# Cumulative gate sums as TensorE products, and the scan's inverse blocks turned on VectorE and placed by Pool

## The chip, the core and the metric

The kernel runs on one core of one Trainium2 chip, in one launch. The metric is the device time of that core in microseconds: the median of repeated executions, 3512.65 us over three runs (3505.86 to 3517.88). One more execution was profiled; it took 3506.29 us. Engines are named as the profile names them: PE is TensorE's matmul row and PEld its weight loads, DVE is VectorE, ACT is ScalarE, POOL is GpSimd, SP is the queue that issues most DMAs.

## What is computed

Two layers of a diffusion trunk over 1024 latent tokens and 256 context tokens of width 1024, all in float32. Layer 0 mixes with pooling and neighbourhood attention, layer 1 with a bidirectional RWKV-7 recurrence; each is followed by a squared-ReLU MLP. The change lies in layer 1. For each direction and each of 16 heads of width 64 the reference does:

```
decay = exp(-exp(-softplus(-w_raw) - 0.5));  a = sigmoid(...);  k_d = k * (1 + (a - 1) * k_a)
S = S * w_t - (S kk_t) (kk_t * a_t) + v_t k_t        # one token after the other, context first
y_t = S r_t
...
bonus = sum(r * (k_d[0] + k_d[1]) * r_k, per head) * v
```

The recurrence is evaluated in chunks of 64 tokens. Within a chunk the decays enter through cumulative sums of their logarithms, and the coupling of a chunk's tokens through the inverse of a unit triangular 64x64 matrix, one for each chunk, direction and head.

## The kernel before

Layer 1's recurrence has two stages that the change touches.

**Features (`l1_scan_features`).** The work goes over 40 units `u`: five spans of 256 tokens (the context first, then four latent spans), each with eight groups of 128 channels (`hp`, two heads). The order is written out by hand, one iteration per unit, in which the steps of several units are interleaved: `decays(u+2)` puts the low-rank gate products on PE, `gates(u+2)` takes two tanh per direction on ACT (decay gate `sg`, key gate `th`; the reverse direction is written back to front) and adds 1 to `sg`, `norms(u+2)` spreads the key norms on PE, `sums(u+2)` forms the cumulative sum of `sg` over each chunk with a VectorE scan along 512 columns (line 1327; `smask` holds a 0 at each chunk's start) and scales the keys, `exps(u+1)` takes both exponentials on ACT, `keys(u+1)` scales the key gate on ACT, `scaled(u)` multiplies everything into the tile F on VectorE (lines 1357 to 1389) and stores it, `scores(u-1)` puts chunk products on PE and stores them to `ls`, and `bonuses(u-1)` adds the bonus sums (line 1413, two products of 2 columns a unit). Between them `value_mm`, `value_in` and `value_out` compute the value projection, 24 matmuls a unit. From the ninth unit on, 2.2 slots of the first inversions are taken from a generator in each iteration.

**The inversions (`scan_blocks`, `scan_invert`).** The diagonal 32x32 blocks of 2 chunks x 2 directions x 8 head pairs x 2 heads x 2 blocks are inverted together, 128 of them, one to a partition: tile M holds the blocks, X starts as identities, and 31 rounds of a product and a subtraction on VectorE (lines 1511 and 1515) leave the inverse. There are ten such blocks `b`; the first two are done during the features, the other eight in the background of the scan. Finished, X and a transposed copy of it (line 1518) are stored to the scratch tensors `lt` and `ltt`.

**Scan (`l1_scan`).** Twenty steps `s`, in each of which both directions `d` advance by one chunk. A step's PE work is a chain: `chain_x`, `chain_u`, `chain_s`, with the readouts and with the scores of the next step `n = s + 1` in four groups between them. A score group (line 1626) goes to one of three PSUM buffers of the pool `scps`, is copied in part by ACT (line 1632) and masked into ZQ by DVE (line 1634). The state SS is updated on DVE (lines 1734, 1738) and carried by ACT (line 1748). `load_blocks` and `load_inverses` fetch the inverses from the scratch: two loads a step for ZT (line 1595) and four for TT (line 1603), where 32 partitions hold a block's rows, so that each packet has 128 bytes. `compose1` and `compose2` (lines 1653, 1667) build the off-diagonal 32x32 part in PSUM of the pool `chps`, which has two buffers and also serves the chain.

What is not a step's own work comes from a generator `background()`: the inversions, then the loads and splits of the output weights and the first rows of the readout. `fill()` is called 16 times a step and draws `pace/2` slots: 2.1/2 until step 2, then 2.45/2, and 1/2 once the inversions are done. The loads of the next inversion (8 DMAs, line 1497) are issued at the 17th of a block's 31 rounds. Pools `M` and `X` have two buffers each; after the inversions their space takes output weights (`readout_weight`). All DMAs named here go through SP, in program order.

Of the kernel before, what the change touches and what calls it, by code (L numbers as in the profile page):

```python
# [58 lines left out]
class Trunk:  # L59
# [983 lines left out]
    def l1_features(self):  # L1043
# [14 lines left out]
        smask = cp.tile([128, 512], BF16, name="smask")  # L1058
        hb = cp.tile([128, 32], F32, name="hb")
        kac = cp.tile([128, 8], F32, name="kac")  # L1060
        rkbd = cp.tile([128, 8, 2], F32, name="rkbd")
# [3 lines left out]
        def scan_constants():  # L1065
            nc.vector.memset(smask, 1.0)
            nc.vector.memset(smask.rearrange("p (c t) -> p c t", t=CH)[:, :, 0:1], 0.0)
# [6 lines left out]
            for e in range(2):  # L1074
                s = slice(e * 64, e * 64 + 64)
                nc.vector.tensor_scalar(out=rkbd[s, :, e], in0=rk[s], scalar1=0.5, scalar2=None, op0=ALU.mult)
# [9 lines left out]
            self.sfc = smask, hb, kac, rkbd, sel, nln2  # L1086
# [108 lines left out]
    def l1_scan_features(self, es, xv, wv0):  # L1195
# [8 lines left out]
        knp = self.pool(es, "sfk", 1, PSUM)  # L1204
        bps = self.pool(es, "sfb", 1, PSUM)
        smask, hb, kac, rkbd, sel, nln2 = self.sfc
# [42 lines left out]
        def value_in(u):  # L1249
            vt = vp.tile([128, 256], F32, tag="vt", name="vt", bufs=1)  # L1250
            nc.scalar.copy(out=vt, in_=vps[u])
            vps[u] = vt

        def value_out(u):
# [5 lines left out]
            v = vp.tile([128, 2, 128], F32, tag="v", name="v", bufs=1)  # L1260
# [42 lines left out]
        def gates(u):  # L1303
# [4 lines left out]
            for d, ps in enumerate(w.pop("pw")):  # L1308
                for i, dst in ((0, sg), (1, th)):
                    c = 16 * i + d * 8 + hp  # L1310
                    nc.scalar.activation(
                        out=dst[:, d, ::-1] if d else dst[:, d], in_=ps[:, i], func=AF.Tanh, scale=0.5, bias=hb[:, c:c + 1]
                    )
            nc.scalar.activation(out=sg, in_=sg, func=AF.Copy, bias=1.0)
            w["sg"], w["th"] = sg, th

        def norms(u):
            t0 = units[u][0]
            ps = U[u]["kn"] = knp.tile([128, n], F32, tag="kn", name="kn")
            nc.tensor.matmul(out=ps, lhsT=sel[:, units[u][1]], rhs=self.rn[:, t0:t0 + n], start=True, stop=True)  # L1320

        def sums(u):
            w = U[u]
            hp = units[u][1]
            sg = w.pop("sg")
            w["cum"] = tp.tile([128, 2, n], F32, tag="cum", name="cum", bufs=2)
            nc.vector.tensor_tensor_scan(  # L1327
                out=fl(w["cum"]), data0=smask, data1=fl(sg), initial=0.0, op0=ALU.mult, op1=ALU.add
            )
# [4 lines left out]
        def exps(u):  # L1334
# [4 lines left out]
            nc.scalar.activation(out=pe[:, :, 1:], in_=cu(w["cum"]), func=AF.Exp, scale=-0.5 * DECAY)  # L1339
            nc.scalar.activation(out=w["cum"], in_=w["cum"], func=AF.Exp, scale=0.5 * DECAY, bias=nln2)  # L1340
# [8 lines left out]
        def scaled(u):  # L1349
# [6 lines left out]
            for d in range(2):  # L1356
                nc.vector.scalar_tensor_tensor(  # L1357
                    out=th[:, d], in0=th[:, d], scalar=1.0, in1=rv(kkt, d), op0=ALU.add, op1=ALU.mult
                )
            nc.vector.tensor_tensor(out=F[:, :, 2], in0=cu(th), in1=cu(iv), op=ALU.mult)  # L1360
            for d in range(2):
                cs = slice(d * nch, d * nch + nch)
                rk3 = (lambda x: c3(x)[:, ::-1, ::-1]) if d else c3
                nc.vector.tensor_tensor(out=F[:, cs, 1], in0=rk3(kkt), in1=pe[:, cs, 0:CH], op=ALU.mult)  # L1364
            for d in range(2):
                nc.vector.tensor_tensor(out=kd[:, d], in0=kd[:, d], in1=rv(w["x"][:, 0], d), op=ALU.mult)
            for d in range(2):
                cs = slice(d * nch, d * nch + nch)
                kap = F[:, cs, 3, ::-1] if d else F[:, cs, 3]
                nc.vector.tensor_tensor(out=kap, in0=c3(kd[:, d]), in1=c3(iv[:, d]), op=ALU.mult)  # L1370
# [15 lines left out]
            if lat:  # L1386
                ks = w["ks"] = tp.tile([128, n], F32, tag="ks", name="ks", bufs=1)
                nc.vector.tensor_tensor(out=ks, in0=kd[:, 0], in1=rv(kd[:, 1], 1), op=ALU.add)
# [17 lines left out]
        def bonuses(u):  # L1406
            w = U.pop(u)
            t0, hp = units[u]
            if w["lat"]:
                if hp == 0:  # L1410
                    self.bp = lps.tile([128, 2, 16], F32, tag="bp", name="bp")
                for j in range(2):
                    nc.tensor.matmul(
# [836 lines left out]
```

## Time and profile before

| | us |
|---|---|
| median of three runs | 3512.65 |
| profiled execution | 3506.29 |
| its span, first to last instruction | 3504.5 |
| PE busy | 3280.3 (94%) |
| PEld busy | 2737.5 (78%) |
| DVE busy | 2043.3 (58%) |
| ACT busy | 1439.4 (41%) |
| POOL busy | 307.6 (9%) |

The page gives shares over the whole span; the two stages of the change are 1859 to 2174 us and about 2184 to 2637 us of it, and there VectorE is far fuller than 58%. A row of instructions reads: line, engine, operation, tile written and tiles read, shape, count, then busy time and mean duration, then the idle time of the engine ahead of them and who ended it. A row of stretches gives for each engine the busy time and the number of instructions, then the clock that TensorE was granted, the busy share of the 16 DMA engines and what they moved.

### The profile page before, as it was taken

How to read it: one execution, taken by the hardware profiler on the slowest of the kernel's cores; microseconds unless marked ns; L12 is line 12 of the kernel's file. 1: busy time of each engine (PE TensorE's matmuls, PEld its weight loads, DVE VectorE, ACT ScalarE, POOL GpSimd, SP SyncE). 2: the span in 40 equal slices, each digit the busy share in tenths (PEclk: the TensorE clock that was granted, in tenths of full speed). 3: DMA queues.
4: the chain of work that ended last, by engine and by line, in shares of the span. 5: the costliest groups of instructions: out<-in, count | busy, mean ns of one | idle time of the engine just before them, and what ended most of it. 6: DMA issues, size and time to landing. Idle time of an engine off the chain costs nothing. (4 is left out here: it accounts for less than half of the span.)

```text
span 3504.5 us, 62351 instructions
## 1 busy us (share of the span) xinstructions
PE 3280.3 (94%) x25466; PEld 2737.5 (78%) x25466; DVE 2043.3 (58%) x3903; ACT 1439.4 (41%) x2743; POOL 307.6 (9%) x396
## 2 busy tenths in 40 slices
PE   8999989999999999989997877899998899999998
PEld 4787767888888889867887776788887788888887
DVE  4255555343444444486757989799766734444446
ACT  4244456312121212166767665566664531221212
POOL 0010110000001000013530000000021100000000
PEclk9999999999999999999999888899999999999999
DMA  8432243322222211143226777898883411111112
GB/s 280 150 94 88 90 137 124 104 76 87 79 79 91 79 43 43 43 141 95 79 70 177 232 229 230 182 209 205 227 219 120 157 48 49 46 46 47 49 49 78
DMA packets 462189, 409.10 MB, mean 117 GB/s; under 512 B 151584, under 2 KB 401312, under 8 KB 461904
## 3 DMA queue, kind: packets, MB, share of 16 engines
q1 hardware_dynamic: 449024, 368.22, 36.0%
q0 software_dynamic: 10560, 35.14, 2.9%
q8 instruction: 200, 3.28, 0.4%
q10 hardware_dynamic: 2320, 1.77, 0.2%
q14 instruction: 85, 0.70, 0.1%
HBM read 292.54 MB, written 112.49 MB: 116 GB/s over the span
## 5 line engine op out<-in xcount | busy, mean ns | idle before, releaser
L916 DVE TENSOR_TENSOR yacc<-yps,yacc 128x512 f32<-128x512 f32 x540 | 369.7, 690 | 304.1 <-PE yps L93 303.7
L74 ACT CAST wh<-st 128x1024 fp32r<-128x1024 f32 x160 | 165.1, 1049 | 761.3 <-PE yps L93 557.8
L93 PE MATMUL yps<-wh,xh 128*128 128x512 f32 x1152 | 453.2, 393 | 3.2 <-DVE yacc L916 1.5
L93 PE MATMUL yps<-wh,xl 128*128 128x512 f32 x1152 | 448.6, 390 | 0.7 <-DVE xl L75 0.7
L93 PE MATMUL yps<-wl,xh 128*128 128x512 f32 x1152 | 449.0, 390 | 0.0
L75 DVE TENSOR_TENSOR wl<-st,wh 128x1024 fp32r<-128x1024 f32 x160 | 194.3, 1229 | 278.2 <-ACT wh L74 278.1
L93 PE MATMUL acc<-h2h,wh 128*128 128x426 f32 (+3 forms) x768 | 274.4, 357 | 3.0 <-ACT y L671 3.0
L93 PE MATMUL acc<-h2h,wl 128*128 128x426 f32 (+3 forms) x768 | 273.3, 356 | 0.0
L93 PE MATMUL acc<-h2l,wh 128*128 128x426 f32 (+3 forms) x768 | 273.0, 355 | 0.0
L93 PEld LDWEIGHTS yps<-wh,xh 128*128 128x128 f32 x1152 | 216.2, 188 | 71.2 <-DVE yacc L916 12.1
L93 PEld LDWEIGHTS yps<-wh,xl 128*128 128x128 f32 x1152 | 216.2, 188 | 47.8 <-DVE xl L75 2.3
L93 PEld LDWEIGHTS yps<-wl,xh 128*128 128x128 f32 x1152 | 216.4, 188 | 44.7 <-issue 1.7
L898 DVE TENSOR_TENSOR r<-r 128x428 f32<-128x428 f32 (+4 forms) x164 | 102.4, 624 | 240.2 <-ACT r L897 240.2
L93 PE MATMUL acc<-mh,wh 128*128 128x256 f32 (+1 forms) x640 | 215.6, 338 | 4.3 <-ACT mh L74 4.2
L93 PE MATMUL acc<-ml,wh 128*128 128x256 f32 (+1 forms) x640 | 214.8, 336 | 0.0
L93 PE MATMUL acc<-mh,wl 128*128 128x256 f32 (+1 forms) x640 | 214.1, 335 | 0.0
L93 PE MATMUL acc<-h2bh,wh 128*128 128x512 f32 (+3 forms) x544 | 211.3, 388 | 1.4 <-ACT wh L74 0.7
L93 PE MATMUL acc<-h2bl,wh 128*128 128x512 f32 (+3 forms) x544 | 211.1, 388 | 1.3 <-DVE h2bl L288 1.3
L93 PE MATMUL acc<-h2bh,wl 128*128 128x512 f32 (+3 forms) x544 | 210.8, 388 | 0.3 <-DVE wl L75 0.3
L897 ACT ACTIVATE r<-acc 128x428 f32<-128x428 f32 (+4 forms) x164 | 89.1, 543 | 291.0 <-PE acc L93 272.0
L93 PEld LDWEIGHTS acc<-h2h,wh 128*128 128x128 f32 x768 | 144.2, 188 | 15.9 <-issue 5.1
L1626 PE MATMUL sc<-FT 64*128 64x192 f32 (+1 forms) x1280 | 144.6, 360 | 11.3 <-DVE ZQ L1641 4.9
(319 smaller groups left out, 6849.5 us busy)
## 6 DMA issues: line engine op xcount, KB each, us to landing
st<-in_mlp_w SPq DMA_DIRECT2D x128, 512.0 KB
ft<-F SPq DMA_DIRECT2D x64, 512.0 KB
FT<-ft SPq DMA_DIRECT2D x128, 256.0 KB
adas<-in_ada_w POOLq DMA_DIRECT2D x112, 256.0 KB, 3.9
adas<-in_ada_w SPq DMA_DIRECT2D x80, 256.0 KB
x<-x SPq DMA_DIRECT2D x28, 512.0 KB
bias<-in_bias SPq DMA_DIRECT2D x64, 192.0 KB
ls<-ls SPq DMA_DIRECT2D x80, 128.0 KB
```

Of the source, the lines that this page charges most:

```text
L74: self.nc.scalar.copy(out=hi, in_=src)
L75: self.nc.vector.tensor_tensor(out=lo, in0=src, in1=hi.bitcast(F32), op=ALU.subtract)
L93: self.nc.tensor.matmul(out=ps, lhsT=lhs[x], rhs=rhs[y], start=first and i == 0, stop=last and i == 2)
L897: nc.scalar.activation(out=r, in_=ps, func=AF.Relu)
L898: nc.vector.tensor_tensor(out=r, in0=r, in1=r, op=ALU.mult)
L916: nc.vector.tensor_tensor(out=yacc[t][:, n], in0=ps, in1=yacc[t][:, n], op=ALU.add)
L1626: nc.tensor.matmul(out=p4[:, j, e, f], lhsT=F[st[e], 2 * g + j, 3:5].rearrange("p a t -> p (a t)"), rhs=F[st[e], 2 * g + j, f], start=True ...
```

## The change

Features: the decay gate is turned on PE in four 128x128 transposes, the +1 is added by ACT on the way back from PSUM, and four float32 products with a triangle of ones (two 64x64 triangles on the diagonal of `tri`) give the sums, straight in the channels' layout. The exponentials read them from PSUM. The bonus is accumulated over the eight channel groups in one PSUM tile of 16 rows, and turned at the end. The key gate `th` is no longer written back to front; instead the products of `scaled` read it reversed, and those of both directions are merged where they can be. `keys(u+1)` moves behind `scores`, `bonuses`, `turned` and `norms`.

```diff
+        def turned(u):
+            sg = fl(U[u]["sg"]).rearrange("p (b t) -> p b t", t=128)
+            ps = bps.tile([128, 4, 128], F32, tag="tr", name="sgt")
+            for b in range(4):
+                nc.tensor.transpose(out=ps[:, b], in_=sg[:, b], identity=self.ident)
+            nc.scalar.activation(out=sg, in_=ps, func=AF.Copy, bias=1.0)
         def sums(u):
-            nc.vector.tensor_tensor_scan(
-                out=fl(w["cum"]), data0=smask, data1=fl(sg), initial=0.0, op0=ALU.mult, op1=ALU.add
-            )
+            ps = w["sum"] = cmp.tile([128, 2, n], F32, tag="cum", name="cum")
+            for b in range(4):
+                nc.tensor.matmul(out=fl(ps)[:, b * 128:(b + 1) * 128], lhsT=sg[:, b], rhs=tri, start=True, stop=True)
...
-            for d in range(2):
-                nc.vector.scalar_tensor_tensor(
-                    out=th[:, d], in0=th[:, d], scalar=1.0, in1=rv(kkt, d), op0=ALU.add, op1=ALU.mult
-                )
-            nc.vector.tensor_tensor(out=F[:, :, 2], in0=cu(th), in1=cu(iv), op=ALU.mult)
+            nc.vector.scalar_tensor_tensor(out=th, in0=th, scalar=1.0, in1=both(kkt), op0=ALU.add, op1=ALU.mult)
...
+                nc.vector.tensor_tensor(out=F[:, cs, 2], in0=rk3(th[:, d]), in1=c3(iv[:, d]), op=ALU.mult)
...
-                for j in range(2):
-                    nc.tensor.matmul(
-                        out=self.bp[:, j, 2 * hp:2 * hp + 2], lhsT=w["ks"][:, j * 128:(j + 1) * 128], rhs=rkbd[:, hp], start=True, stop=True
-                    )
+                nc.tensor.matmul(out=fl(self.bp)[0:16], lhsT=rkbd[:, hp], rhs=w["ks"], start=hp == 0, stop=hp == 7)
```

Scan: only the first two blocks still go through the scratch, read in eight loads each. From the third on, X itself is kept in `ready` and turned by two VectorE block transposes at the start of step `2b - 1`, the step before the block is first used (`n = 2b`). Pool copies the turned rows into TT at the start of each step; ZT is a view. A block's partitions are ordered anew, so that its loads are 16 of 8 partitions. `compose2` takes its PSUM from `scps`.

```diff
-                for d in range(2):
-                    p0 = t * 64 + bl * 32 + d * 16
-                    dma(out=M[p0:p0 + 16], in_=self.ls[b // 2, d, :, :, blk, (2 * b + t) % 4, blk].rearrange("h e s t -> (h e) s t"))
+                for e in range(2):
+                    for d in range(2):
+                        p0 = e * 64 + bl * 32 + t * 16 + d * 8
+                        dma(out=M[p0:p0 + 8], in_=self.ls[b // 2, d, :, e, blk, (2 * b + t) % 4, blk])
...
+            def turn_inverses(b):
+                X = ready.pop(b)[1]
+                rows = ip.tile([128, 32, 32], F32, tag="BK", name="YR")
+                columns = zs.tile([128, 32, 32], F32, tag="YC", name="YC", bufs=1)
+                nc.vector.transpose(out=columns.rearrange("p m r -> p r m"), in_=X)
+                nc.vector.transpose(out=rows.rearrange("p m t -> p t m"), in_=X.rearrange("p r t -> p t r"))
+            def place_inverses(s):
+                for q in range(4):
+                    bl = q % 2
+                    nc.gpsimd.tensor_copy(out=dh(TT[quads[q], :, :, bl * 32:bl * 32 + 32]), in_=rows[quads[q]])
...
-                p2 = chps.tile([128, 2, 8, 32], F32, tag="ch", name="p2")
+                p2 = scps.tile([128, 2, 512], F32, tag="sc", name="p2")[:, 0].rearrange("p (d h t) -> p d h t", d=2, h=8)
...
                     for i, _ in enumerate(self.scan_invert(ip, b, *blocks)):
-                        if i == 16 and b + 1 < NSTEP // 2:
-                            blocks = self.scan_blocks(ip, b + 1, nc.sync.dma_start)
+                        if i >= 16 and nxt is None and b + 1 < NSTEP // 2 and b - 1 not in ready:
+                            nxt = self.scan_blocks(ip, b + 1, nc.sync.dma_start)
                         yield
+                    ready[b] = blocks
+                    while nxt is None and b + 1 < NSTEP // 2:
+                        if b - 1 not in ready:
+                            nxt = self.scan_blocks(ip, b + 1, nc.sync.dma_start)
+                        yield
...
-                self.readout_weight_load(0)
...
-                for k in (1, 2, 3):
+                for k in (0, 1, 2):
                     self.readout_weight_load(k)
...
-                self.readout_weight(1)
+                while ready:
+                    yield
+                for k in range(2):
+                    self.readout_weight(k)
+                    yield
...
                     load_values(n, d)
+                    if not d and n % 2 == 0:
+                        while n >= 4 and n // 2 not in ready:
+                            next(bg)
+                        first_inverses(n // 2) if n < 4 else turn_inverses(n // 2)
+                    if not d and s:
+                        place_inverses(n)
                     chain_x(s, d)
```

More of the change, by code (lines that the diff above doesn't have):

```diff
@@ L1085, in scan_constants @@
             nc.vector.memset(nln2, -LN2)
-            self.sfc = smask, hb, kac, rkbd, sel, nln2
+            self.sfc = tri, hb, kac, rkbd, sel, nln2
         self.open_wpool(es, 1, 2)
@@ L1203, in l1_scan_features @@
         lps = self.pool(es, "sfl", 1, PSUM)
-        knp = self.pool(es, "sfk", 1, PSUM)
+        cmp = self.pool(es, "sfc", 1, PSUM)
         bps = self.pool(es, "sfb", 1, PSUM)
-        smask, hb, kac, rkbd, sel, nln2 = self.sfc
+        tri, hb, kac, rkbd, sel, nln2 = self.sfc
         half = (slice(0, 64), slice(64, 128))
@@ L1311, in gates @@
                     nc.scalar.activation(
-                        out=dst[:, d, ::-1] if d else dst[:, d], in_=ps[:, i], func=AF.Tanh, scale=0.5, bias=hb[:, c:c + 1]
+                        out=rv(dst[:, d], d and i == 0), in_=ps[:, i], func=AF.Tanh, scale=0.5, bias=hb[:, c:c + 1]
                     )
-            nc.scalar.activation(out=sg, in_=sg, func=AF.Copy, bias=1.0)
             w["sg"], w["th"] = sg, th
@@ L1434, in l1_scan_features @@
                 gates(u)
+                turned(u)
+                sums(u)
                 norms(u)
-                sums(u)
-            exps(0)
+                scaled_keys(u)
+                if u == 0:
+                    exps(u)
             keys(0)
@@ L1464, in l1_scan_features @@
                 if u + 2 < nu:
+                    turned(u + 2)
                     norms(u + 2)
+                if u + 1 < nu:
+                    keys(u + 1)
                 if v < nu:
@@ L1581, in load_values @@
                 W[s]["D"][d] = D_
-            quarter = lambda x, s, bl, e: x.rearrange("(s b c e) i t -> i s b e c t", s=2, b=2, e=2)[:, s % 2, bl, e]
+            quads = [slice(q * 32, q * 32 + 32) for q in range(4)]
+            turned, ready = {}, {}
             def load_blocks(s, e):
@@ new lines, in first_inverses @@
+            def first_inverses(b):
+                rows, columns = ip.tile([128, 32, 32], F32, tag="BK", name="YR"), zs.tile([128, 32, 32], F32, tag="YC", name="YC", bufs=1)
+                for t, src in ((rows, lt_[b]), (columns, ltt_[b])):
+                    for q in quads:
+                        nc.sync.dma_start(out=t[q], in_=src[q].rearrange("m i t -> i m t"))
+                turned[b] = rows, columns
+            def turn_inverses(b):
[4 more added lines that the diff above has]
+                nc.vector.transpose(out=rows.rearrange("p m t -> p t m"), in_=X.rearrange("p r t -> p t r"))
+                turned[b] = rows, columns
@@ L1793, in l1_scan @@
                 nc.gpsimd.memset(W[0]["D"][d][0:64], 0.0)
+            first_inverses(0)
             for e in range(2):
                 load_blocks(0, e)
-                load_inverses(0, e)
+            nc.gpsimd.memset(TTs[1], 0.0)
+            for s in range(2):
+                place_inverses(s)
             for d in range(2):
```

98 lines of the change are left out of this document (50 added, 48 removed).

## The prediction, made before the changed kernel was run

> **What bounds the kernel now.** I read the page first, then the trace by stage. The change touches two stages: the RWKV features (about 1859 to 2174 us, 40 units of 256 tokens by 128 channels) and the scan (about 2184 to 2637 us, 20 steps). The busy times by stretch are context units, latent units, scan steps with the inversion behind them, and scan steps after it:
>
> ```profile
> core 0: us, PE busy (x) PEld busy (x) DVE busy (x) ACT busy (x) POOL busy (x), PEclk, DMA share, GB/s
> 1859.00:1907.00 48.00, 43.32 (x500) 40.08 (x499) 42.75 (x92) 43.65 (x98) 1.93 (x10) 1.00 0.69 209
> 1907.00:2174.00 267.00, 210.06 (x2157) 191.44 (x2155) 248.27 (x607) 169.87 (x379) 6.45 (x34) 0.90 0.76 225
> 2284.00:2500.00 216.00, 197.37 (x4915) 175.58 (x4916) 197.09 (x491) 140.18 (x270) 4.43 (x8) 0.95 0.87 204
> 2500.00:2616.00 116.00, 107.53 (x2749) 95.71 (x2744) 77.53 (x101) 82.96 (x154) 28.08 (x12) 0.96 0.89 241
> ```
>
> Units are counted by the one key activation that each has, in the same two feature stretches:
>
> ```profile
> L1347 ACT ACTIVATE kd<-th,kac,cols 128x512 f32<-128x512 f32 x9 | 7.3, 816 | 0.8 <-DVE F L1370 0.8
> L1347 ACT ACTIVATE kd<-th,kac,cols 128x512 f32<-128x512 f32 x32 | 26.1, 814 | 44.6 <-DVE ks L1388 35.7 <-DMA FT<-ft 6.3 <-DVE ks L1389 2.2
> ```
>
> A latent unit thus takes 267/32 = 8.35 us, in which VectorE (DVE) works 248.3/32 = 7.76 us (93%) and TensorE (PE) 6.56 (79%): VectorE bounds it. A context unit takes 48/9 = 5.33, and there TensorE is the fullest together with ScalarE (43.3 and 43.7 of 48). In the scan TensorE and VectorE are both at 91% while the inversion runs. After it VectorE falls to 67%, yet TensorE stays at 93%, so TensorE is the scan's floor. A step's length does not fall when VectorE empties: nine state updates, two to a step, lie between 2405.0 and 2495.1, which is 90.1/4 = 22.5 us a step.
>
> ```profile
> L1738 DVE TENSOR_TENSOR SS<-SS,pcs x9: 691/692/693, 2405.0 to 2495.1; 128x512 f32<-128x512 f32 x9
> L1515 DVE TENSOR_TENSOR X<-X,tmp 128x112 f32<-128x112 f32 (+15 forms) x183 | 63.1, 345 | 6.3
> L1511 DVE TENSOR_TENSOR tmp<-X,M 128x112 f32<-128x112 f32 (+15 forms) x183 | 62.2, 340 | 2.9
> L1634 DVE TENSOR_TENSOR ZQ<-sc,masks 128x512 f32<-128x512 f32 x79 | 54.0, 685 | 8.7 <-ACT TM L1632 8.6
> L1518 DVE COPY M<-X 128x1024 f32<-128x1024 f32 x6 | 6.4, 1062 | 0.1
> ```
>
> **Features: the sums move to TensorE.** The scan leaves VectorE. Of a unit on TensorE these rows show the small work, in order of time, ahead of the value projection:
>
> ```profile
> L1327 DVE TENSOR_TENSOR_SCAN cum<-smask,sg 128x512 f32<-128x512 bf16 x40 | 48.8, 1220 | 6.1 <-ACT sg L1314 5.4
> ...
> 1994.05 0.44 PE L1259 MATMUL vtr<-ident,vt 128*128 128x128 f32 x2 [1.46 <-ACT vt L1251]
> 1994.42 1.15 PE L1398 MATMUL lp<-F 64*64 64x64 f32 x32
> 1995.50 0.61 PE L1413 MATMUL bp<-rkbd,ks 128*128 128x2 f32 x4
> 1995.96 0.36 PE L1320 MATMUL kn<-rn,sel 128*128 128x256 f32 x1
> 1996.16 0.28 PE L93 MATMUL acc<-mh,wh 128*128 128x256 f32 x1
> ```
>
> Removed: 1.22 us of VectorE a unit. The merged products over both directions save about 0.15 more (estimate: two pairs of 256 columns become single ones of 512, while one of 512 is split). VectorE would need 7.76 - 1.37 = 6.4 us in a latent unit. Added on TensorE: four transposes and four f32 products against the triangle, 128 columns each. Two transposes hold the queue 0.37 us up to the next group, so four about 0.6. The bonus product shows what an f32 product with full 128x128 weights costs: four instructions in 0.46 us, 0.115 each, two instructions a product. The triangle's products have 128 moving columns instead of 2; 0.115 is the lower bound and 0.185 the upper (a transpose of 128 columns, 0.37/2, the change to the next group counted in). I take 0.115, since eight products in a row change group only once: 8 x 0.115 = 0.9, and 1.5 at the upper bound. The new bonus product (two passes of 256 columns, 16 weight columns) costs about what the old four instructions did. Sum: 0.6 + 0.9 = 1.5 us a unit. Everything else in this stage goes together at nothing: the +1 on ScalarE has the same size from PSUM, the norm product only changes its pool, the value copies share a ring, and the mask's fills give way to two small DMAs.
>
> So what is late next is TensorE. Latent units: busy 6.56 + 1.5 = 8.06, from which the pipelined tails go (the rows above start 0.1 to 0.2 before the one ahead ends, in five groups, so up to 0.8): 7.3 to 8.06; I take 7.75 and gain 0.6 x 32 = 19 us. Context units: 43.3/9 = 4.8 busy of 5.33, 0.5 is free, so 1.5 - 0.5 = +1.0 each, 9 units: +9 us. The bounds are +4 and +13.
>
> **The block loads double.** A 64x64 inverse block is now read by 16 DMAs of half the size where 8 were, on the same SP queue. Two of the stalls that such loads cause today, once in the features and once in the scan:
>
> ```profile
> 2056.18 4.45 SPq L1497 DMA_DIRECT2D M<-ls  x8
> 2064.76 0.19 DVE L1511 TENSOR_TENSOR tmp<-X,M 128x31 f32<-128x31 f32 x1 [5.35 <-DMA xt<-ascr]
> 2201.23 5.27 SPq L1497 DMA_DIRECT2D M<-ls  x8
> 2209.69 0.19 DVE L1511 TENSOR_TENSOR tmp<-X,M 128x31 f32<-128x31 f32 x1 [6.84 <-DMA M<-ls]
> ```
>
> Eight issues take 4.45 us, 0.55 each, and VectorE goes on 3.2 to 4.1 us after the last. Sixteen take 8.9, so data are there 12 to 13 us after the first issue instead of 8.5. In the features this lengthens two stalls of VectorE by 4.4 each: +9 us at most, if nothing absorbs it. Features in all: -19 + 9 + 9 = -1 us.
>
> **Scan: the inverses no longer go through the scratch.** Removed from SP: six loads a step (TT and ZT) and two stores a block; from the DMA engines, the smallest packets:
>
> ```profile
> DMA packets 172289, 94.94 MB, mean 210 GB/s; under 512 B 120481, under 2 KB 160373, under 8 KB 172193
> ...
> TT<-lt SPq DMA_DIRECT2D x78, 64.0 KB
> ...
> M<-ls SPq DMA_DIRECT2D x64, 64.0 KB
> ...
> ZT<-ltt SPq DMA_DIRECT2D x39, 64.0 KB
> ```
>
> TT and ZT are 117 x 512 = 59,904 packets of 128 bytes, half of the small ones. Added on VectorE: two block transposes of 128x1024 a block for one transposing copy of 1.06 us (the L1518 row). I price each like that copy, net +1.06 x 8 blocks = 8.5 us, between 0 and twice that; it sits at the start of a step, ahead of the masks, and VectorE has 22.5 - 20 = 2.5 us free in such a step (below), so 0 to 4 us end up on the path; I take 1. The Trainium skill, "VectorE: DVE Perf Modes", section "The three transpose paths", gives 311 ns for 128x128 in bf16 on VectorE; eight of them would be an estimated 2.5 us a transpose, and by that the net would be 3.9 us a block. No run here shows it.
>
> What can be gained is bounded by TensorE's idle time from 2284 to 2616: 18.6 + 8.5 = 27 us. The rows that the change removes from it:
>
> ```profile
> PE p L1667 <- DVE SS L1734: 9.6, 6, 2.4
> ...
> 2303.53 5.93 DMA FT<-ft
> 2309.47 5.08 DMA TT<-lt
> ...
> 2502.39 7.73 DMA FT<-ft
> ```
>
> The second composition moves to the score pool, so it no longer waits for a state update queued behind the inversion: up to 9.6. The DMA pieces in the chain are 18.7 us, mostly beside busy engines; I take a third. Together -16.
>
> **The new wait.** X is now kept until its block is turned, X has two buffers, and so the loads of block b+1 wait for the turn of block b-1, which happens at the start of step 2b-3. The schedule is static: 16 fills a step at 1.225 background slots, 19.6 a step, 32 slots a block. Counting slots through the loop: today the loads are issued 16 slots before the inversion that needs them, and the last block ends in step 13. With the change blocks 6 to 9 start two slots after their loads (steps 7, 9, 11, 13) and block 5 four slots after (step 5); the last ends in step 14. Two slots are under 2.5 us, the loads need 12. I place the first issue 2.5 us into the step (behind the outputs, values and keys that SP sends there), so data are there at 14.4. VectorE arrives after the turn (2 x 1.06) and two masks (2 x 0.685), at about 5.5: it stands still for 9 us. Queued behind on VectorE: the masks of the third and fourth score group, the state updates, all later inversion. Waiting for those: the score buffers (three), ScalarE's carry of the state and with it all its copies. TensorE has work until it needs the third group's buffer again. These are the ends of one half step of the chain, which has the first composition inside that the half with the wait does not have:
>
> ```profile
> 2383.73 1.08 PE xp L1678 x32
> 2384.81 1.50 PE sc L1626 x16
> ...
> 2387.39 1.13 PE p L1653 x64
> ...
> 2392.46 0.85 PE sc L1626 x8
> ```
>
> Such a half lasts 9.58 - 1.13 = 8.45 us; with the next xp (1.08) and one score group (0.75) TensorE needs the buffer at 10.3. It gets it at 14.4 + two short inversion pairs (0.19 a product, 0.8) + 0.69 = 15.9. That is 5 us for each of four blocks, and 3 for block 5, whose start leaves two slots more: +23, and no fewer than 0. In return the inversion is spread over two steps a block instead of 1.6: VectorE's load falls from 22 to 8 x 0.685 + 4 x 0.69 + (31 x 0.685 + 2.1)/2 = 20 us a step, which is why the lag does not pile up.
>
> **POOL's copies.** Four copies of 32x512 a step go to Pool, which has nothing to do there. Their length is between the memset rate and that of its two-input rows, 0.5 to 1.2 us each: half of its 1.05 us for a 128x1024 memset, and half of 2.36 (row below); half a step covers them. Three rows speak of a cost elsewhere: the same 128x128 subtraction on VectorE, once beside a Pool operation and once alone.
>
> ```profile
> L1501 POOL MEMSET X<- 128x1024 f32 x7 | 7.3, 1047 | 239.2 <-DMA lt<-X 104.4 <-DVE ZQ L1641 63.8 <-DVE X L1515 35.5
> ...
> 2607.35 2.36 POOL L1990 TENSOR_TENSOR y<-y,ld 128x1024 f32<-128x1024 f32 x1 [6.34 <-DVE gst L1933]
> 2607.71 2.15 DVE L75 TENSOR_TENSOR gs<-gst,gs 128x128 fp32r<-128x128 f32 x1 [0.36 <-ACT gs L74]
> 2630.43 0.29 DVE L75 TENSOR_TENSOR gs<-gst,gs 128x128 fp32r<-128x128 f32 x1 [3.26 <-ACT gs L74]
> ```
>
> The first ended with Pool's operation, 1.9 us late. The inversion's operations are of that kind (two inputs from SBUF), so four copies could hold VectorE 2 to 4.8 us a step. In the five steps with the new wait that is hidden; in ten others VectorE's 2.5 us free cover most: +3. The Trainium skill, "SBUF — State Buffer", section "SBUF: two separate sides", says that a Pool operation and a VectorE one with two SBUF inputs lock each other out for the whole instruction; the rows agree.
>
> **Ends.** At the start SP has 38 issues ahead of the first step's values instead of 34 (8 first loads and 8 more block loads, 12 fewer TT/ZT): 4 x 0.55, +2. At the end the background finishes about one step later, and the loads of the first output weights fall behind the loop:
>
> ```profile
> 2610.27 2.44 SPq L1906 DMA_DIRECT2D ld<-in_rw_wo  x3
> ...
> 2614.66 1.05 ACT L74 CAST rwoh<-ld 128x1024 fp32r<-128x1024 f32 x1 [0.89 <-DMA ld<-in_rw_wo]
> ```
>
> They take 4.4 us to the first cast; ScalarE waits for that with the last step's copies behind it: +4, between 0 and 8. Scan in all: -16 + 1 + 23 + 3 + 2 + 4 = +17.
>
> Total: -1 + 17 = +16 on 3506.3 us, the profiled execution's own time (span 3504.5). That execution lies 6.4 below the median of the three runs, 3512.65, against which I state the forecast: 3528 us.
>
> **Rivals.** (1) The forecast, the load wait decides: slower, 0.40. (2) The load wait is hidden. It turns at 4.5 us: if the sixteen land within 10 us of the step's start (SP runs ahead now that six loads a step are gone), TensorE never sees it. Then 23 falls away, the features' stall too: 16 - 23 - 9 = -16, 3497 us; with the latent units at 7.3 instead of 7.75 another -14. For: half of the small packets are gone, and SP sends six loads a step less and four more. Against: the outputs' stores keep SP in step with TensorE. Chance 0.28. (3) TensorE gives back in the features what VectorE saves, and half of the wait is absorbed: within 10 us of 3512.65; 0.22. It is also what happens if the sums merely change engines. (4) Pool's copies decide: as in the stretched row, VectorE's two-input operations stand still while a copy runs, 4 x 1.2 = 4.8 us in each of ten steps, 2.3 after the 2.5 that are free: +23 where the forecast has 3, 3548 us; 0.10. The one stretched row bears it out, but for an operation at least twice as long as a copy. (The exclusive lock in the page on SBUF named above is this mechanism.)
>
> **Numbers.** Under 0.3%, 10.5 us, a measurement of this kernel cannot tell a change from none. Slower is 0.40 + 0.10, no change 0.22, faster 0.28. The range leaves out a tenth at either end: from 3490 (rival 2 with part of the faster units) to 3552 (just above rival 4). The likeliest case's own range is 3514 to 3545.
>
> **What would show it.** Right: latent units of about 7.75 us with TensorE ahead of VectorE, context units of 6.3; in steps 7, 9, 11 and 13 a first inversion product after 7 to 10 us of idle VectorE put down to M, and a longer TensorE gap after it; the waits of L1667 on the state update gone; a DMA share clearly under 0.87 in the scan. Wrong: no VectorE idle before a block's first product, or steps of 21 us throughout, would leave rival 2; two-input operations of VectorE stretched beside Pool's copies in every step, rival 4.

## The result and the profile after

The changed kernel takes 3561.11 us (median of four runs, 3557.52 to 3566.33) where the kernel before takes 3515.25 in the same series: 1.0137 times as long, 95% interval 1.0122 to 1.0151. That is 46 us lost where 15 were forecast. The profiled execution has a span of 3555.6 us, 51 more than before. The page of the changed kernel, its busy rows and some of the 40 slices:

```profile
span 3555.6 us, 63286 instructions
PE 3322.9 (93%) x25890; PEld 2771.4 (78%) x25890; DVE 2040.0 (57%) x3834; ACT 1436.9 (40%) x2743; POOL 361.0 (10%) x476
...
PE   8999889999999999989989987788978899999998
...
DVE  4255555344444444596656986987876734444446
```

The PE slices of the kernel before:

```profile
PE   8999989999999999989997877899998899999998
```

In sum VectorE is as busy as before (2040.0 against 2043.3 us): the features took work from it and the scan gave it back. The scan is slices 25 to 30, where PE reads 7 or 8 in five of the six; in the kernel before it is slices 26 to 30, which read one 8 and four 9. Windows of the changed kernel: the features' first nine units (the eight of the context and one more), the 30 units behind them, and the scan from 2284 us to the end of the last inversion.

```profile
core 0: us, PE busy (x) PEld busy (x) DVE busy (x) ACT busy (x) POOL busy (x), PEclk, DMA share, GB/s
1861.00:1922.00 61.00, 58.38 (x672) 56.18 (x673) 40.76 (x90) 49.54 (x112) 2.05 (x11) 1.00 0.65 194
1922.00:2171.00 249.00, 222.68 (x2441) 200.97 (x2439) 213.05 (x533) 163.72 (x368) 6.38 (x33) 0.96 0.78 234
2284.00:2558.00 274.00, 234.06 (x5629) 205.44 (x5625) 225.71 (x515) 160.56 (x311) 29.92 (x50) 0.91 0.60 139
```

The first nine units take 61 us, 6.8 each, PE nearly full. The next 30 take 249 us; without the two that hold stalls for block loads (16.3 and 13.4 us from one key activation to the next) that is 7.8 each. Counted in the same way, from one key activation to the next, the kernel before takes 5.9 us in the first units and 8.4 in the later ones, with stalls of 12.5 and 12.7. In the scan the DMA share falls to 0.60, and still TensorE idles 40 of 274 us. The update of the state brackets the loop (count, then nanoseconds, then first and last start); the first two rows are of the changed kernel, the others of the kernel before:

```profile
L1780 DVE TENSOR_TENSOR SS<-SS,pcs x36: 691/692/1751, 2234.2 to 2653.6; 128x512 f32<-128x512 f32 x36
L1780 DVE TENSOR_TENSOR SS<-sp,pcs x2: 692/692/693, 2213.2 to 2222.0; 128x512 f32<-128x512 f32 x2
...
L1738 DVE TENSOR_TENSOR SS<-SS,pcs x36: 691/692/694, 2234.7 to 2614.7; 128x512 f32<-128x512 f32 x36
L1738 DVE TENSOR_TENSOR SS<-sp,pcs x2: 692/692/692, 2212.7 to 2221.5; 128x512 f32<-128x512 f32 x2
```

So the loop, from the first state (2213.2) to the last (2653.6), takes 440.4 us; in the kernel before (2212.7 to 2614.7) it takes 402.0. After the last state follow 902.0 us where 889.8 did. Of the 51 us, 38 lie in the loop and 12 behind it. The timeline of the changed kernel at the step that turns block 4 shows the new wait (start, length, engine; idle time and releaser in brackets):

```profile
2358.66 1.96 DVE L1634 STREAM_TRANSPOSE YC<-X 128x1024 f32<-128x1024 f32 x1
...
2360.48 1.99 DVE L1635 STREAM_TRANSPOSE YR<-X 128x1024 f32<-128x1024 f32 x1
...
2361.17 8.56 SPq L1521 DMA_DIRECT2D M<-ls  x16
...
2362.36 1.26 DVE L1676 TENSOR_TENSOR ZQ<-sc,masks 128x512 f32<-128x512 f32 x2
...
2367.55 0.92 PE L1668 MATMUL sc<-FT 64*128 64x192 f32 x8
...
2373.22 0.19 DVE L1533 TENSOR_TENSOR tmp<-X,M 128x31 f32<-128x31 f32 x1 [9.60 <-DMA M<-ls]
...
2374.80 1.65 PE L1668 MATMUL sc<-FT 64*128 64x192 f32 x8 [6.33 <-DVE ZQ L1676]
```

Two transposes of 2 us, two masks, then VectorE stands 9.6 us until the sixteen loads have landed, and TensorE 6.3 us behind it. This is the picture that the prediction drew, except that each transpose takes twice the time. It comes four times: VectorE stands 9.6, 8.4, 8.1 and 7.0 us (the profile puts the third down to a load of FT), TensorE 6.3, 5.1, 3.7 and 2.9. VectorE's groups in the loop (busy and mean ns of one, then idle before), the last two rows from the loop of the kernel before:

```profile
L1537 DVE TENSOR_TENSOR X<-X,tmp 128x31 f32<-128x31 f32 (+15 forms) x248 | 90.9, 367 | 8.5
L1533 DVE TENSOR_TENSOR tmp<-X,M 128x31 f32<-128x31 f32 (+15 forms) x248 | 87.7, 354 | 46.0 <-DMA M<-ls 24.9 <-DMA FT<-ft 8.1 <-DMA lng<-in_rw_lng 8.1
...
L1635 DVE STREAM_TRANSPOSE YR<-X 128x1024 f32<-128x1024 f32 x8 | 16.0, 2001 | 0.0
L1634 DVE STREAM_TRANSPOSE YC<-X 128x1024 f32<-128x1024 f32 x8 | 15.6, 1955 | 0.0
...
L1515 DVE TENSOR_TENSOR X<-X,tmp 128x31 f32<-128x31 f32 (+15 forms) x248 | 85.0, 343 | 8.5
L1511 DVE TENSOR_TENSOR tmp<-X,M 128x31 f32<-128x31 f32 (+15 forms) x248 | 84.0, 339 | 11.4 <-DMA M<-ls 6.8
```

The inversion's subtraction and product (343 and 339 ns before) have become slower too, 367 and 354. The timeline says where, a product and a subtraction of the same 128x156 shape one after the other:

```profile
2378.19 0.31 DVE L1533 TENSOR_TENSOR tmp<-X,M 128x156 f32<-128x156 f32 x1
...
2378.41 2.60 POOL L1645 COPY TT<-YR 32x512 f32<-32x512 f32 x4 [12.02 <-PE up L1728]
...
2378.53 0.65 DVE L1537 TENSOR_TENSOR X<-X,tmp 128x156 f32<-128x156 f32 x1
```

The product takes 0.31 us ahead of Pool's copies, the subtraction 0.65 beside them (0.32 elsewhere in this loop, without a copy). So three suspects stand in the loop: the late load (the prediction's new wait), the transposes, and Pool's copies (rival 4 of the prediction).

### The profile page after: what moved, and what is told of

Its sections match the earlier page's. It is cut to its first block, busy times and chain, and to the rows that moved or that the text cites. A ratio compares the mean times of both kernels' runs of the same rounds, so it can differ in the third digit from the quotient of the medians.

```text
span 3555.6 us, 63286 instructions
## 1 busy us (share of the span) xinstructions
PE 3322.9 (93%) x25890; PEld 2771.4 (78%) x25890; DVE 2040.0 (57%) x3834; ACT 1436.9 (40%) x2743; POOL 361.0 (10%) x476
```

## The experiments

The table gives each kernel's median, its ratio to the kernel before in the same series with the interval, and from its trace the first state, the loop (first to last state) and the rest behind it, in us. Median and ratio rest on four to ten executions; the last three columns are of one profiled execution each, which can lie some us from its kernel's median.

| kernel | median | ratio | first state | loop | behind |
|---|---|---|---|---|---|
| before | 3515.25 | 1 | 2212.7 | 402.0 | 889.8 |
| after | 3561.11 | 1.0137 [1.0122, 1.0151] | 2213.2 | 440.4 | 902.0 |
| e1 eight loads | 3545.95 | 1.0086 [1.0063, 1.0108] | 2208.9 | 436.4 | 898.4 |
| e2 early loads | 3535.84 | 1.0061 [1.0046, 1.0076] | 2213.4 | 421.1 | 898.0 |
| e4 features only | 3507.47 | 0.9979 [0.9969, 0.9990] | 2210.3 | 400.9 | 892.6 |
| e5 scan only | 3570.87 | 1.0151 [1.0134, 1.0167] | 2220.7 | 449.8 | 898.8 |
| e6 turn twice | 3564.47 | 1.0147 [1.0130, 1.0164] | 2213.7 | 445.1 | 902.3 |
| e7 copies twice | 3563.63 | 1.0141 [1.0126, 1.0156] | 2214.2 | 445.5 | 901.9 |
| e9 p2 moved | 3505.53 | 0.9976 [0.9963, 0.9988] | 2206.3 | 402.6 | 895.2 |
| e10 weights later | 3535.04 | 1.0061 [1.0046, 1.0076] | 2217.9 | 419.9 | 899.0 |
| e11 X first | 3537.36 | 1.0068 [1.0046, 1.0090] | 2216.5 | 412.6 | 903.6 |
| e12 scalar places | 3580.35 | 1.0189 [1.0166, 1.0213] | 2217.1 | 457.3 | 902.3 |
| e13 X first, scalar | 3577.15 | 1.0180 [1.0153, 1.0206] | 2214.2 | 460.8 | 902.0 |
| e14 plain turn | 3530.12 | 1.0055 [1.0035, 1.0074] | 2218.3 | 413.7 | 903.2 |
| e15 no inverse loads | 3493.95 | 0.9948 [0.9929, 0.9966] | 2205.6 | 392.1 | 891.1 |
| e16 no copies | 3519.26 | 1.0022 [1.0010, 1.0034] | 2217.1 | 400.3 | 901.2 |
| e17 no turn | 3518.54 | 1.0013 [0.9999, 1.0026] | 2213.8 | 399.1 | 898.6 |
| e18 neither | 3510.08 | 0.9993 [0.9980, 1.0007] | 2215.1 | 393.0 | 900.0 |
| e19 rescue | 3544.36 | 1.0086 [1.0071, 1.0100] | 2209.2 | 434.8 | 898.6 |

**The parts by themselves.** e4 has the gate sums alone, e5 the turned inverses alone.

> The kernel before with the first part of the change alone: gate sums on TensorE, the scan as before. From the changed kernel's features stage (309.3 us where it was 314.9) I expect 3 to 6 us less than the kernel before: 3510 (3505 to 3515). If the features' two longer waits pushed something into the scan, it would be no faster than 3515.

> The kernel before with the second part of the change alone: the inverses turned by VectorE and placed by Pool, the features as before. If the two parts add up, this one carries the whole loss: 3565 (3558 to 3572), the loop at about 440 us and the stretch after the last state at about 902. If the two parts work on one another (the new load of the features' sums changes when the first five inverses are ready), it stands below 3555.

Features 8 us faster, scan 55 slower; the sum, 47, is the change. The two parts add up.

**The load.** e1 merges each pair of loads; e2 issues them where the kernel before does, and only X's two memsets, now in a function of their own, wait for the turn:

```
-                    for d in range(2):
-                        dma(out=M[p0:p0 + 8], in_=self.ls[b // 2, d, :, e, blk, (2 * b + t) % 4, blk])
+                    dma(out=M[p0:p0 + 16], in_=self.ls[b // 2, :, :, e, blk, (2 * b + t) % 4, blk].rearrange("d h s t -> (d h) s t"))
```

```
+                        if i == 16 and b + 1 < NSTEP // 2:
+                            nm = self.scan_blocks(ip, b + 1, nc.sync.dma_start)
                         if i >= 16 and nxt is None and b + 1 < NSTEP // 2 and b - 1 not in ready:
-                            nxt = self.scan_blocks(ip, b + 1, nc.sync.dma_start)
+                            nxt = nm, self.scan_identity(ip)
```

> The changed kernel with the load of each block's M (L1521) as 8 transfers of 16 partitions where it had 16 of 8; the bytes and the moment of the first are the same. Theory A (the loads of M stand between two blocks of the inversion, and VectorE has no slack to make up what it waits): SyncE's issue of a block's loads falls from 8.6 us to about 4.3, VectorE waits about 4 us less in each of blocks 6 to 9, the scan loop falls from 440 us by 12 to 18 and the time from 3561 to about 3545 (3540 to 3550). Theory B (the waits are absorbed; the block transposes and the lock of Pool's copies cost the time): within 4 us of 3561. Theory C (more packets in flight cost more than the issue): no change or slower.

> The changed kernel with the loads of M issued at round 17 of the block ahead, as the kernel before does it; only X's two memsets on Pool still wait until the turn has read the old X. All else (transposes, Pool copies, gate sums) stays. Theory A (the late load is the cost): no first inversion product waits for M, the steps of 27, 25, 29 and 30 us become 22 to 24, the loop falls from 440 us to 408 to 418, and the time from 3561 to about 3534 (3525 to 3542); the rest of the loss, some 10 us, is the transposes (4 us a block where 2 were reckoned), and stays. Theory B (transposes and the Pool lock fill VectorE): 3552 to 3561, and the wait turns into dense VectorE time. The stretch after the last state, 902 us, should fall too by a few us if its length follows from the inversion that ends late.

Both came out as theory A says: 15 and 25 us less. In e2 the loop is 19 us shorter (421 us, not quite the 408 to 418 expected), and the wait for M in front of blocks 6 to 9 is gone (the waits of e2 between 2284 and 2558; what is left waits for X, refilled on Pool behind the copies):

```profile
DVE tmp L1538 <- POOL X L1529: 11.3, 4, 2.8
```

But e2 is still 28 us slower than the features alone, although no load of M is late there.

**Transposes and copies, doubled.** e6 loops twice over the two transposes of e2, e7 over Pool's four copies of each step.

> The changed kernel with the early loads of M (as e2, 3535.8 us), and every block transpose issued twice into the same tile: 16 more of 1.96 to 2.01 us on VectorE in the loop, 31.7 us in all; the output is the same. Theory A (the loop goes at VectorE's pace, so that its added work shows at nearly full price; of e2's remaining loss against the features alone, 28 us, the transposes are some 20): 3556 to 3568. Theory B (a turn stands in front of work that waits anyway): within 8 us of e2.

> As e2, with Pool's four copies of a step issued twice (80 more of 0.6 us, 48 us of Pool). In e2's loop VectorE's operations with two inputs from SBUF took some 13 us longer in sum than in the kernel before, with the copies beside them. Theory A (the lock is a minor part): VectorE's work grows by as much once more, the time by 6 to 14 us over e2, 3542 to 3550. Theory B (rival 4 of the prediction: VectorE stands still for all of a copy): +30 to +48, 3566 or more. If copies cost nothing beside VectorE: within 3 us of e2.

The second set of transposes cost 28.6 us of the 31.7 that it keeps VectorE busy; the second set of copies 27.8 of its 48 on Pool, twice the upper end of theory A and just under the point of theory B. Together with e2's other losses these prices come to more than e2 has lost. So the first sets were taken out of e2: e16 places no copies and e17 turns nothing from the third step and third block on, e18 neither; e15 is e9 without the scratch loads. All four compute with stale inverses.

> e2 (3535.8 us) without Pool's copies from step 2 on: TT keeps the diagonal blocks of steps 0 and 1, so the output is not the reference's. VectorE's operations with two inputs should fall back to 339 and 343 ns (some 13 us in sum) and the waits for X on Pool go (11 us). If the first set of copies costs what the second did (e7, 27.8): 3506 to 3512. If VectorE's slack covers half of it: 3518 to 3526. If the copies cost nothing in e2: 3533 or more.

> e2 without the block transposes: from step 4 on the inverses of block 1 are placed again, so the output is not the reference's; Pool's copies stay. VectorE has 31.7 us less to do. If the first set costs what the second did (e6, 28.6): 3504 to 3510. If a part is covered by VectorE's waits for ScalarE (19 us in e2, 35 in the kernel before): 3512 to 3522.

> e2 with neither transposes nor copies (the output is not the reference's): the change with its inverses for nothing. If the costs of e16 and e17 add up it would be near 3485; I expect them to overlap, since TensorE becomes the pace (14 us of PE waits on VectorE's masks in e2 go): 3495 to 3505, of which the stretch after the last state keeps its 898 us or more, since output weight 0 still waits for X. It is the lowest that the way chosen here can reach, to be held against e15.

> e9 (features part and p2 in the score pool, inverses through the scratch; 3505.5 us) with the loads of TT and ZT left out from step 2 on: these steps compute with the inverses of steps 0 and 1, so the output is not the reference's. 54 of 60 such loads a direction of the packets of 128 bytes go, the copies and stores of the inversion stay. It measures the relief that the change can bring: if the DMAs of the inverses hold the loop, as the prediction's last 6 us of relief said, 3495 to 3500; if SyncE's queue and the packets are hidden, within 3 us of 3505.5. Below 3490 would mean that the relief is far larger than I reckoned, and is what hides the sum of the prices of e6 and e7.

e18 came 5 us above its range and e15 1 us below one of its own; e16 and e17 came as one of their cases says. By the medians the transposes alone (e16) cost 9 us over e18, the copies alone (e17) 8, both (e2) 26. The loops say the same more sharply, each in one execution (e17's was the fastest of its ten, 5 us below its median): neither 393.0, transposes alone 400.3, copies alone 399.1, both 421.1; alone 7 and 6 us, together 28. Where this happens shows in eight steps of the middle, from the seventh state of direction 0 to the fifteenth, in which each kernel does the same work on TensorE. Rows in the order neither (e18), transposes alone (e16), copies alone (e17), both (e2):

```profile
core 0: us, PE busy (x) PEld busy (x) DVE busy (x) ACT busy (x) POOL busy (x), PEclk, DMA share, GB/s
2336.72:2504.84 168.12, 158.14 (x4096) 140.54 (x4096) 141.05 (x348) 116.60 (x224) 3.33 (x6) 0.98 0.72 174
2347.36:2516.76 169.40, 158.83 (x4096) 140.92 (x4096) 155.60 (x356) 116.83 (x224) 4.43 (x8) 0.98 0.71 172
2342.71:2513.51 170.80, 159.47 (x4102) 141.27 (x4100) 147.38 (x349) 117.35 (x226) 25.43 (x40) 0.98 0.71 171
2349.58:2532.76 183.18, 164.77 (x4096) 146.05 (x4096) 159.02 (x357) 116.95 (x224) 25.32 (x40) 0.94 0.67 159
```

In the first three TensorE is 93 to 94% busy, and 15 or 6 us more of VectorE's time lengthen the eight steps by only 1.3 and 2.7 us. With both, VectorE works 18 us more and the steps take 15 us more: either one fits into the slack, both do not. Of these 15, about 7 are TensorE's own busy time, at a granted clock of 0.94 where the others have 0.98; whether the lower clock follows from the waits is not shown. And with its inverses for nothing the whole loop (393.0) runs no faster than that of the kernel before without its inverse loads (e15, 392.1); the relief is there, 10 us against e9, and no more.

e12 moves the copies of e2 to ScalarE, e13 does so with e11's order (below):

```
-                    nc.gpsimd.tensor_copy(out=dh(TT[quads[q], :, :, bl * 32:bl * 32 + 32]), in_=rows[quads[q]])
+                    nc.scalar.copy(out=dh(TT[quads[q], :, :, bl * 32:bl * 32 + 32]), in_=rows[quads[q]])
```

> As e2, with the four copies of a step on ScalarE where Pool had them: 48 us more on ScalarE, which is busy 273 of 429 us in the loop, no lock with VectorE, and X's memsets on Pool no longer behind copies. Theory A: VectorE's products and subtractions fall back to 339 and 343 ns (from 351 and 366), about 13 us, and the X waits go, 11 us; against that the copies lie in ScalarE's queue ahead of the chain's own, 2.4 us a step at most. 3520 to 3535. If Pool's copies cost nothing (theory B turned round): ScalarE's added work shows, 3540 or more.

> As e11, with the copies on ScalarE as in e12. The memsets are ahead of nothing now, so by theory A it equals e12 within 4 us: 3520 to 3535; a gain over both e11 and e12 by over 6 us would mean that the two costs add to one another. If ScalarE becomes the pace: slower than e11.

Both missed: 44 and 41 us slower than e2. VectorE's groups in the loop of e12:

```profile
L1542 DVE TENSOR_TENSOR X<-X,tmp 128x31 f32<-128x31 f32 (+15 forms) x248 | 85.0, 343 | 8.5
L1538 DVE TENSOR_TENSOR tmp<-X,M 128x31 f32<-128x31 f32 (+15 forms) x248 | 84.0, 339 | 11.3 <-DMA M<-ls 6.6
```

The means are those of the kernel before to the nanosecond, so Pool's copies had stretched them. TensorE's longest wait in the same loop, and the longest of ScalarE (sum, times, longest):

```profile
PE up L1733 <- ACT XS L1726: 68.2, 16, 11.6
ACT TT L1650 <- DVE YR L1640: 42.6, 8, 11.4
```

ScalarE waits 42.6 us with a copy for the transposes, about the 44 that were lost, and everything of the chain queues behind that wait. Of the two places tried Pool is the better one for an operation that waits long; its price is VectorE's longer operations beside it.

**X, strides, a rescue.** e11 refills X right behind the transposes, ahead of the copies; e14 lets both transposes read and write in plain order (blocks in the wrong places); e19 joins e1, e2 and e11 and lets the transposes write plainly, with the strides moved to the readers, so that its output is right. Of e19's edit, the transposes:

```
-                nc.vector.transpose(out=columns.rearrange("p m r -> p r m"), in_=X)
-                nc.vector.transpose(out=rows.rearrange("p m t -> p t m"), in_=X.rearrange("p r t -> p t r"))
-                turned[b] = rows, columns
+                nc.vector.transpose(out=columns, in_=X)
+                nc.vector.transpose(out=rows, in_=X.rearrange("p r t -> p t r"))
+                turned[b] = rows.rearrange("p t m -> p m t"), columns.rearrange("p r m -> p m r")
```

> As e2 (3535.8 us), with X's two memsets for the block after next issued to Pool right behind the turn, ahead of Pool's four copies, where e2 has them behind the copies. In e2 the first product of a block still waited for X on Pool, 11.3 us in four waits; with the copies doubled (e7) 23.5. Theory A (VectorE's time is the loop's time): these 11.3 us go, 3524 to 3530. If the wait is absorbed: within 3 us of e2.

> As e2, with both block transposes reading X and writing their tiles in plain order (contiguous in the free dimension), so that the blocks are not the ones of the reference: a measure of the transpose by itself. In e2 they take 1.96 and 2.01 us with strides of 32 elements. If the stride costs: about 1.1 us each, as the plain copy of that size (1.06), and the time falls by 12 to 15 us, 3521 to 3525. If the transpose of float32 has this price: 1.9 to 2.0 us each and the time within 3 us of e2.

> The change with what the runs so far ask for, and the reference's output: early loads of M (e2), in eight DMAs (e1), X refilled ahead of the copies (e11), and both transposes writing their tile in plain order (e14), with the strides moved to the readers (the weights' side of the first composition and Pool's copies; the second transpose still reads X with a stride of 32 elements). From e2's 3535.8: some 5 us less at the start (first state at about 2209 instead of 2213 to 2218), 6 to 9 from the transposes, 0 to 8 from X: 3514 to 3525, no better than the features part alone (3507). If the strides cost the readers what they cost VectorE: 3526 to 3532. If the start does not move, the doubled loads were not its cause.

e11's loop is 8.5 us shorter, as expected, but the time is e2's: the stretch ahead of the loop and the one behind it are longer by 3.1 and 5.6 in this execution, the first of which lies ahead of any difference between the two (e10, too, has e2's code there and starts 4.5 later). e14 gains 6 us where 12 to 15 were expected, and its interval overlaps e2's. Its transposes in the loop:

```profile
L1639 DVE STREAM_TRANSPOSE YC<-X 128x1024 f32<-128x1024 f32 x8 | 9.9, 1236 | 0.0
...
L1640 DVE STREAM_TRANSPOSE YR<-X 128x1024 f32<-128x1024 f32 x8 | 9.6, 1202 | 0.0
```

VectorE's groups in the loop of e19, and below them Pool's copies there:

```profile
L1541 DVE TENSOR_TENSOR X<-X,tmp 128x31 f32<-128x31 f32 (+15 forms) x248 | 105.3, 425 | 8.5
L1537 DVE TENSOR_TENSOR tmp<-X,M 128x31 f32<-128x31 f32 (+15 forms) x248 | 98.0, 395 | 8.5 <-DMA M<-ls 3.8
...
L1639 DVE STREAM_TRANSPOSE YR<-X 128x1024 f32<-128x1024 f32 x8 | 15.4, 1924 | 0.0
L1638 DVE STREAM_TRANSPOSE YC<-X 128x1024 f32<-128x1024 f32 x8 | 9.9, 1235 | 0.0
```

```profile
L1651 POOL COPY TT<-YR 32x512 f32<-32x512 f32 x72 | 76.8, 1067 | 113.5 <-PE up L1734 46.3 <-DVE YR L1639 35.5 <-DMA YR<-lt 28.4
```

The rescue failed, 8.5 us slower than e2, though its loop starts 4 us sooner. A stride of 32 elements costs a transpose 0.7 us whether it is read or written; handed to Pool it makes the copy 1.07 us instead of 0.67, and the inversion's operations grow to 425 and 395 ns. In sum the two groups are 34 us above their length without Pool's copies, where e2's are 9. Pool's time alone does not explain that: e7, with 97 us of plain copies in the loop, has 18. TensorE pays as well: the first composition, which now reads strided weights, is busy 36.0 us in e19's loop (222 ns each) and 23.8 in e2's (192 ns). No run parts the two readers.

**Relief and tail.** e9 is e4 with p2 in the score pool; e10 puts the casts of output weights 0 and 1 behind the last step's first products.

> The features part alone (e4, 3507.5 us) with one more edit of the change: the second composition p2 takes its PSUM from the score pool. This is the relief of the prediction by itself: the waits of p2 on the state update (9.6 us in the kernel before) go. If TensorE is the pace of the loop: 3498 to 3502. If VectorE is (theory A): within 3 us of 3507, since the wait only moves.

> As e2, with the casts of output weights 0 and 1 put behind the last step's first products and their copies on ScalarE (and the loads of weights 3 and 4, which need the same ring, with them); the loads of 0 to 2 stay. In e2 TensorE stands 12.7 us before the last step while ScalarE waits 6.3 us for weight 0 ahead of the copies that the products need. If that wait is the tail's loss (898 us after the last state against 890): 3526 to 3530. If the weights are then late for the readout by as much: within 3 us of e2's 3535.8.

e9 stands at 3505.5 where e4 has 3507.5: no relief, within the intervals, though p2's wait on the state is gone from TensorE's list. e10 did nothing for the tail. TensorE's wait for ZQ behind the last state in the kernel before, in the changed kernel, then its longest waits in e10:

```profile
PE xp L1678 <- ACT ZQ L1608: 2.6, 1, 2.6
```

```profile
PE xp L1720 <- ACT ZQ L1650: 12.9, 2, 12.7
```

```profile
PE xp L1725 <- ACT ZQ L1655: 5.6, 2, 5.4
PE yp L1760 <- ACT D L1735: 4.4, 1, 4.4
```

The casts still stand in ScalarE's queue ahead of copies that TensorE needs, now of later ones; the stretch keeps its 899 us.

## Why the prediction was wrong

Its direction and its first mechanism held; the size did not, and the measured time lies above its range. By its steps:

- **Features, −1.** This was −10 for the units and +9 for the doubled loads. The units gave −8 by e4 (0.9979), which keeps eight loads a block. The loads cost 5 to 6: from the first key activation to the last, the five kernels with the new features and eight loads take 302.3 to 305.1 us, seven of those with sixteen 308.7 to 310.9, and e5 320.1 where the kernel before has 314.9. The units' lengths came near, 7.8 us in the later ones (7.75) and 6.8 in the context (6.3), but partly by luck. The prediction divided 48 us by nine key activations that span only eight units, so a context unit took 5.9 us before and not 5.33. TensorE's busy time rose by 0.7 us a unit and not 1.5, and VectorE's fell by 0.9 and not 1.37 (e4's page against that of the kernel before, over 40 units).
- **The load wait, +23.** Right: 25 us by e2, 15 of which e1's halved issue gives back; VectorE's idle 7.0 to 9.6 us (9 forecast), TensorE's 2.9 to 6.3 (5).
- **The turns, "I take 1", and Pool, "+3".** This is the step that failed: 4 us together, where e18 and e2 measure 26. Each was sized by itself against "VectorE's 2.5 us free". In the eight steps of the middle each alone does nearly fit, at 1.3 and 2.7 us; over the whole kernel they cost 9 and 8 alone, and some 8 more together, because the same slack was spent twice. Two sizes behind it were off as well: a transpose takes 1.96 and 2.01 us and not 1.06, so that the net is 23 us of VectorE and not 8.5; and beside a copy of 0.65 us an operation of the inversion takes twice its time. The Trainium skill, "VectorE: DVE Perf Modes", section "The three transpose paths", led to an estimate of 2.5 us a transpose; of the two figures it was the nearer. The lock that the Trainium skill, "SBUF — State Buffer", section "SBUF: two separate sides", describes is borne out by the rows above, and by e12 and e16, where without Pool's copies the inversion's times fall back to 343 and 339 or 338 ns.
- **"The lag does not pile up."** It did. VectorE's load a step is near the 20 us reckoned (e2 in its eight steps: 159.02 us, 19.9 a step), but it is not spread evenly: the step with the turn holds 4 us more. The four steps of the changed kernel with a wait for M are 20 us longer in sum than e2's (29.0, 25.5, 29.9 and 24.8 us against 22.2, 22.6, 22.4 and 21.7), and the four between them give nothing back, so that of VectorE's 33 us of waiting 20 show.
- **Relief, −16.** p2's 9.6 gave nothing clear of the intervals (e9), the DMAs 10 to 12 where 6 were set (e15). That the sum comes near is luck.
- **Ends, +2 and +4.** Behind the loop +8 to +12 (e2 898.0 and the changed kernel 902.0, against 889.8). The loss is there without transposes and copies, too (e18, 900.0 against e15's 891.1). The first load of the output weights is issued 4.4 us ahead of the last state in the kernel before and 7.5 us behind it in e2. Ahead of the loop, the kernels with the new features and eight loads a block have their first state at 2205.6 to 2210.3 (e4, e9, e15, and e1 and e19 of the changed scan), those with sixteen at 2213.2 to 2218.3 (twelve profiles); without the new features it is 2212.7 against 2220.7 (e5). The doubled loads cost some 4 to 8 us up to there, most of it in the features' stalls above.

By medians, along a line of kernels: e4 to e9 −2 (p2), to e15 −12 (loads of the inverses), to e18 +16 (in the profiles 9.5 ahead of the loop and 8.9 behind it), to e2 +26 (transposes and copies together), to the changed kernel +25 (the late load): 54 in all, and −8 for the features makes the 46. Each of these prices holds in its place in the line: the late load, for one, was measured with the transposes and copies in place.

Rival 4 had the right mechanism at the wrong price: in e2 the inversion's operations are 9 us longer in sum (366 and 351 ns for 343 and 339, 248 times each), where 72 copies took 48. What stays open: why e11's shorter loop gave no shorter time beyond the scatter of starts, what in the tail must move, and why e19's operations grew as much as they did. That weight 0 loads late is shown; that it does because X is kept until the last turn and the weight needs its space is argued from the code.

No version with turned inverses beat the kernel before. The version that does is the features part, by itself (0.9979) or with p2 moved (0.9976, 0.9963 to 0.9988).

## What to carry to other kernels

When several small costs are each called covered, add them up against one and the same slack before calling any of them free; a 2x2 of kernels with neither, either and both shows it in four runs. A buffer that is kept longer delays the load that refills it, and the first thing to try is to part the load from what really needs the space. To move an operation off a queue, look first at how long it waits there, and at what its new queue holds behind it.

## What the runs showed of the hardware

A 32x32 block transpose of 128x1024 float32 on VectorE took 1.2 us in plain order (e14) and 1.9 to 2.0 with a stride of 32 elements on either side (e19, e2). Pool's copy of 32x512 took 0.64 to 0.69 us in the mean of a loop with plain reads and 1.07 with strided ones (e19). Beside it VectorE's operations with two inputs from SBUF took up to 2.4 times their time (0.61 us for 0.25, 128x87, e2), and about 1.1 us for 0.2 beside a strided copy (128x31, e19). The masks, which read one input from PSUM, kept theirs: 0.68 us under a copy for their whole length (e2 at 2276.69), and 681 to 685 ns in the mean of every kernel's loop.
